# First mixer of a 1-core transformer kernel: query products moved to VectorE, one exponential for the decayed keys, pooling sums in one POOL run

## The chip, the cores and the metric

The kernel runs on one core of a Trainium2 chip. The metric is the device time of one execution in microseconds (us); the time given for a kernel is the median of its runs. The engines are TensorE (PE), VectorE (DVE), ScalarE (ACT), GpSimd (POOL) and SyncE (SP, which issues the weight loads).

## What is computed

The reference is two transformer blocks on 256 tokens of width 1024. The change lies in the first mixer of the first block, which has two halves: a causal pooling over four windows, and a gated linear recurrence with a per-channel decay.

```python
def causal_multiscale_pool(u):            # four groups of 128 channels, windows 2, 4, 8, 16
    ...
    mean = ...                            # running mean over the window, shorter at the start
    return (mean - uf).astype(u.dtype)

def even_mixer(h, w_in, pool_w, pool_scale, lb, out_gain, w_out):
    z = h @ w_in
    u, q, fz, i, g = jnp.split(z, cuts, axis=-1)
    pooled = causal_multiscale_pool(u.reshape(B_, S_, POOL_GROUPS, POOL_GROUP_DIM))
    a_out = jnp.einsum('bsgc,gcd->bsgd', pooled, pool_w).reshape(B_, S_, POOL_WIDTH) * pool_scale
    fz32 = jnp.clip(fz.astype(jnp.float32), -GATE_CLIP, GATE_CLIP)
    logf = jax.nn.log_sigmoid(fz32) + jnp.log1p(lb * jnp.exp(-fz32))
    k = (1.0 - lb) * jax.nn.sigmoid(-fz32)
    o = hgrn2_chunkwise(hs(q), hs(k), hs(i), hs(logf))
    o = rmsnorm(o, out_gain) * jax.nn.silu(hs(g))
    return jnp.concatenate([a_out, b_out], axis=-1) @ w_out
```

The recurrence's output at token t is the sum over s <= t of v[s] times the inner product of q[t] and k[s], each channel damped by exp of the sum of logf from s+1 to t. The rest of the two blocks (attention, memory attention, feed-forward parts) is untouched.

## The kernel before

Activations lie feature-major: 128 partitions by tokens. Each large product is done as three single-pass matmuls, with weights split in a high and a low part. Weights stream in groups of 128x1024 (512 KB): SP loads a group into one of 6 `raw` buffers, ACT casts it in two halves into `rhi` (line 203), DVE subtracts in two halves into `rlo` (line 241), and PE multiplies (lines 216 to 218 for a projection by columns, 24 matmuls of 256 columns a group). A ring of 7 split groups lies between the splits and PE; the split of group g + 7 becomes possible when PE is done with group g.

The code is one straight trace. A planner reads it before the launch and lays out a fixed order for each engine: at each step the instruction that comes first in the trace among those that are ready by the planner's own times. Every engine then works in its fixed order and waits by semaphores. `after(i, name)` (line 197) adds only an order on one engine. `take` (line 248) traces, before a projection, all splits that the ring allows by then, so they stand ahead of what is traced after.

`even_mixer` computes the recurrence by levels. For c = 1, 2, 4, ..., 128, the second half of each run of 2c tokens takes from the first half. `P` holds log decays summed from the run's start, `Su` those to the run's end; both are 128x1024 (four heads of 256 tokens). `level(c)` (line 724) makes the two operands: Q = exp(P) * q on the odd runs (512 columns, always in the first half of the tile `X`; the exponential on ACT, the product on POOL), and K = exp(Su) * k on the even runs (in `Y`, the exponential on ACT, the product on DVE). Level 1 uses k as it is. `masked(li, Q, K)` (line 708) multiplies them on PE (line 711, 8 products in full float32, shown as x16) and DVE copies by mask into `sT` (line 715). `advance(c)` (line 717) updates Su and P on DVE for the next level. Levels 64 and 128 have their own products (lines 814 and 822).

Beside it stand other jobs: the gate projection `gproj`, the value projection `iproj` (512-column matmuls, lines 318 to 320), the projection `uproj` of the pooling input, and jobs of the memory attention: `mem_start` (mem load, squares, high and low parts), `mem_rstd`, and key and value projections which `fill(n)` (line 538) takes one by one from a list. They are traced between the levels.

`pool_means` (line 753) makes for each of the four groups log2(w) shifted sums, each an add and a copy of the first columns on POOL, with two scratch chunks of `fz` in turn (groups 0 and 2 share one pair, 1 and 3 the other), and then two steps on DVE: a correction of the first 16 columns and the mean minus the input. It is traced between `masked(5, level(16))` and `advance(16)`. `pool_out` (line 770) multiplies the result on PE (line 777).

Elementwise calls go through helpers, so that the profile shows them under the helper's line: `tt` is line 209 (on DVE, or POOL where `self.g` is passed), `stt` line 212, `act` line 191. All units of the mixer are called `u` in the profile.

Of the kernel before, what the change touches and what calls it, by code (L numbers as in the profile page):

```python
# [11 lines left out]
AF = mybir.ActivationFunctionType  # L12
ALU = mybir.AluOpType
# [89 lines left out]
class Kern:  # L103
# [525 lines left out]
    def even_mixer(self):  # L629
        A = self.unit  # L630
        fz, q, k, sg, P, Su, Y = (A() for _ in range(7))
        X = self.maskin
        mem = self.big()
        vt, u = mem.units
        sT = A()
        cross, pw = self.ring(2, 512)
        inv, lbc = self.inv, self.lbc
# [21 lines left out]
        e4, r4, lb = lbc[:, 0:4], lbc[:, 4:8], lbc[:, 8:12]  # L659
# [4 lines left out]
        self.tt(lb, e4, e4, ALU.subtract)  # L664
        self.v.tensor_scalar(lb, lb, 0.0, 1.0, ALU.max, ALU.min)
        self.v.tensor_scalar(r4, lb, -1.0, 1.0, ALU.mult, ALU.add)
        self.g.memset(Su, 0.0)
        self.g.memset(sT, 0.0)

        ps0, ps1 = self.bank(0, 8), self.bank(0, 8)  # L670
# [10 lines left out]
        self.act(X, X, AF.Ln, bias=self.epsc[:, 1:2])  # L681
        self.stt(P, fz, 0.0, X, ALU.min, ALU.subtract)
        self.stt(Y, fz, 0.0, X, ALU.max, ALU.add)
        self.act(k, Y, AF.Exp, scale=-1.0)
        self.act(X, fz, AF.Exp, scale=-1.0)
        for h in range(4):
            c = self.chunk(X, h)
            self.act(c, c, AF.Ln, scale=lb[:, h:h + 1], bias=self.epsc[:, 1:2])
            self.v.tensor_scalar(self.chunk(k, h), self.chunk(k, h), r4[:, h:h + 1], None, ALU.mult)
        self.tt(P, P, X, ALU.add)  # L690
        psq1 = cols(512, 1)
        for j, ps in enumerate((psq0, psq1)):
# [2 lines left out]
        def runs(t, c, odd):  # L695
            return t.rearrange("p (n two c) -> p n two c", two=2, c=c)[:, :, odd]
# [10 lines left out]

        def masked(li, Q, K):
            ps = self.bank(0, 8)
            for b in range(8):  # L710
                self.pe.matmul(ps[:, b * 64:(b + 1) * 64], K[:, b * 128:(b + 1) * 128], Q[:, b * 64:(b + 1) * 64],  # L711
                               start=True, stop=True)
            c = LEVELS[li]
            V = lambda z: z.rearrange("p (n c) -> p n c", c=c)
            self.v.copy_predicated(runs(sT, c, 1), V(mk[:, li - 1]), V(ps))

        def advance(c):
            Pv = P.rearrange("p (s two c) -> p s two c", two=2, c=c)
            Sv = Su.rearrange("p (s two c) -> p s two c", two=2, c=c)
            n = 1024 // (2 * c)  # L720
            self.tt(Sv[:, :, 0], Sv[:, :, 0], Pv[:, :, 1, c - 1:c].to_broadcast([128, n, c]), ALU.add)
            self.tt(Pv[:, :, 1], Pv[:, :, 1], Pv[:, :, 0, c - 1:c].to_broadcast([128, n, c]), ALU.add)

        def level(c):

            Q = X[:, 0:512]
            Qv = Q.rearrange("p (n c) -> p n c", c=c)
            self.act(Qv, runs(P, c, 1), AF.Exp)
            self.tt(Qv, Qv, runs(q, c, 1), ALU.mult, self.g)
            if c == 1:  # L730
                return Q, k
            K = runs(Y, c, 0)
            self.act(K, runs(Su, c, 0), AF.Exp)
            self.tt(K, K, runs(k, c, 0), ALU.mult)
            return Q, Y

        def gproj(j):
# [12 lines left out]

        mh, ml = self.xh, self.xl

        def pool_means():
            for g, w in enumerate((2, 4, 8, 16)):
                src = self.chunk(u, g)
                cur = src
                sh = 1
                bufs = [self.chunk(fz, 2 * (g % 2) + i) for i in range(2)]
                i = 0
                while sh < w:  # L760
                    dst = bufs[i % 2]
                    i += 1
                    self.tt(dst[:, sh:], cur[:, sh:], cur[:, :256 - sh], ALU.add, self.g)
                    self.g.tensor_copy(dst[:, :sh], cur[:, :sh])
                    cur = dst
                    sh *= 2
                self.tt(cur[:, :16], cur[:, :16], inv[:, g * 16:(g + 1) * 16], ALU.mult)
                self.stt(src, cur, 1.0 / w, src, ALU.mult, ALU.subtract)

        def pool_out():  # L770
            pool_out1(0)
            pool_out1(1)
# [14 lines left out]
        diagonal()  # L787
        gproj(0)
        masked(1, *level(1))
        gproj(1)  # L790
        advance(1)
        iproj()
        masked(2, *level(2))
        advance(2)
        uproj(0)
        masked(3, *level(4))
        advance(4)
        uproj(1)
# [2 lines left out]
        self.mem_rstd()  # L801
        self.fill(1)
        masked(5, *level(16))
        pool_means()
        advance(16)
        self.fill(1)
        masked(6, *level(32))
        advance(32)
        self.fill(1)
        pool_out()  # L810
        Q, K = level(64)
        ps = self.bank(0, 8)
        for b in range(8):
            self.pe.matmul(ps[0:64, b * 64:(b + 1) * 64], K[:, b * 128:b * 128 + 64], Q[:, b * 64:(b + 1) * 64],
                           start=True, stop=True)
# [3 lines left out]
        Q, K = level(128)  # L819
# [22 lines left out]
        for j in range(2):  # L842
            c = slice(j * 512, (j + 1) * 512)
# [610 lines left out]
```

## Time and profile before

| | us |
|---|---|
| median of 3 runs | 1805.41 (1805.23 to 1806.15) |
| the profiled execution | 1806.07 |
| its span, first to last instruction | 1804.3 |
| PE busy in it | 1766.9 |
| DVE busy in it | 1243.2 |
| ACT busy in it | 1032.1 |
| POOL busy in it | 113.3 |

The mixer's part with the levels lies between about 44 and 126 us of the span. The page gives each engine's busy time; the waits say who waited for whom; the timeline lists the instructions of one engine in order; the windows give busy time and the granted clock of a stretch (1.00 is 2.4 GHz, 0.50 is 1.2 GHz). Ends of matmuls are modelled; starts are recorded. A row's duration overlaps the next start by about 0.1 us on DVE and ACT.

### The profile page before, as it was taken

Reading aid. Unit: us, or ns where it says so; the run is one execution under the profiler, and the core shown is the slowest. Engines: PE = TensorE matmul, PEld = TensorE weight load, DVE = VectorE, ACT = ScalarE, POOL = GpSimd, SP = SyncE. Lnnn points to the kernel's source line nnn. Section 1 sums busy time; section 2 is a strip of 40 time slices with the busy share of each in tenths; the row PEclk is TensorE's granted clock in tenths of the full one; section 3 lists DMA queues with packets and bytes.
Section 4 is the critical chain, followed back from the end, with each engine's and each line's share of the span. In section 5 each row is a group of like instructions: output and inputs, shape, how many; then the busy total and the mean of one; then the engine's idle time right before and its main releaser. Section 6 shows DMA issues by size and latency. Waiting matters only on the chain.

```text
span 1804.3 us, 36074 instructions
## 1 busy us (share of the span) xinstructions
PE 1766.9 (98%) x14406; PEld 1717.1 (95%) x14406; DVE 1243.2 (69%) x2262; ACT 1032.1 (57%) x2037; POOL 113.3 (6%) x128
## 2 busy tenths in 40 slices
PE   8899999999999999999999999999999999999997
PEld 8889999999889999999999998999999999899997
DVE  8877786557787685557656778766686666876664
ACT  7556565556566465556544667645465455775453
POOL 2420000000000000000000002000010000200000
PEclk9899999999999999999999999999999999999999
DMA  7434445554653435554555554555555555335651
GB/s 284 155 118 141 163 143 209 188 187 158 221 171 127 166 130 189 189 190 153 186 196 184 180 176 135 164 188 187 195 167 187 189 186 177 118 129 188 197 177 36
DMA packets 85625, 307.81 MB, mean 171 GB/s; under 512 B 9680, under 2 KB 10320, under 8 KB 85456
## 3 DMA queue, kind: packets, MB, share of 16 engines
q1 hardware_dynamic: 83952, 300.92, 49.3%
q0 software_dynamic: 640, 3.15, 0.6%
q8 instruction: 112, 1.84, 0.4%
q10 hardware_dynamic: 864, 1.44, 0.2%
q14 instruction: 57, 0.47, 0.1%
HBM read 304.42 MB, written 1.05 MB: 169 GB/s over the span
## 4 chain that ended last, share of the span: by engine, by line
PE 87%; DVE 6%; ACT 3%; issue 1%; POOL 1%; DMA 1%; DVEq 0%; ACTq 0%; SPq 0%; POOLq 0%
PE ps L218 25%; PE ps L216 25%; PE ps L217 25%; DVE rlo L241 2%; ACT u L191 1%; DVE u L212 1%; PE ps L318 1%; PE ps L299 1%; PE ps L300 1%; PE ps L319 1%; PE ps L320 1%; DVE u L209 1%; PE ps L298 1%; DVE xlo L212 1%; PE ps L921 1%
## 5 line engine op out<-in xcount | busy, mean ns | idle before, releaser
L203 ACT CAST rhi<-raw 128x512 fp32r<-128x512 f32 (+1 forms) x1138 | 670.0, 618 | 619.8 <-PE ps L218 582.5
L241 DVE TENSOR_TENSOR rlo<-raw,rhi 128x512 fp32r<-128x512 f32 (+1 forms) x1138 | 764.9, 697 | 328.1 <-ACT rhi L203 323.7
L216 PE MATMUL ps<-xhi,rhi 128*128 128x256 f32 x2560 | 719.9, 281 | 4.7 <-ACT xhi L191 4.0
L218 PE MATMUL ps<-xlo,rhi 128*128 128x256 f32 x2560 | 717.2, 281 | 2.5 <-DVE xlo L212 2.5
L217 PE MATMUL ps<-xhi,rlo 128*128 128x256 f32 x2560 | 715.7, 280 | 0.7 <-DVE rlo L241 0.7
L216 PEld LDWEIGHTS ps<-xhi,rhi 128*128 128x128 f32 x2560 | 482.3, 188 | 8.2 <-ACT xhi L191 5.0
L218 PEld LDWEIGHTS ps<-xlo,rhi 128*128 128x128 f32 x2560 | 481.9, 188 | 4.8 <-DVE xlo L212 4.7
L217 PEld LDWEIGHTS ps<-xhi,rlo 128*128 128x128 f32 x2560 | 482.2, 188 | 1.7 <-DVE rlo L241 1.3
L216 PE MATMUL ps<-u,rhi 128*128 128x256 f32 x1680 | 473.2, 282 | 0.0
L218 PE MATMUL ps<-u,rhi 128*128 128x256 f32 x1680 | 470.2, 280 | 0.0
L217 PE MATMUL ps<-u,rlo 128*128 128x256 f32 x1680 | 470.0, 280 | 0.0
L216 PEld LDWEIGHTS ps<-u,rhi 128*128 128x128 f32 x1680 | 316.4, 188 | 1.0 <-issue 0.7
L218 PEld LDWEIGHTS ps<-u,rhi 128*128 128x128 f32 x1680 | 316.3, 188 | 0.7 <-DVE u L206 0.6
L217 PEld LDWEIGHTS ps<-u,rlo 128*128 128x128 f32 x1680 | 316.5, 188 | 0.4 <-issue 0.2
L209 DVE TENSOR_TENSOR u<-ps,rst 128x512 f32<-128x512 f32 (+1 forms) x129 | 84.0, 656 | 102.2 <-PE ps L218 101.8
L209 POOL TENSOR_TENSOR ssum<-ssum,sqb 128x512 f32<-128x512 f32 x26 | 37.7, 1448 | 1254.0 <-ACT sqb L191 1253.8
L191 ACT ACTIVATE u<-u 128x256 f32<-128x256 f32 (+3 forms) x158 | 86.4, 548 | 36.2 <-PE ps L711 19.4
L206 DVE TENSOR_TENSOR u<-u,u 128x256 fp32r<-128x256 f32 (+2 forms) x128 | 66.7, 521 | 10.2 <-ACT u L203 8.3
L203 ACT CAST u<-u 128x256 fp32r<-128x256 f32 (+2 forms) x128 | 62.0, 484 | 11.2 <-POOL u L1186 7.3
L191 ACT ACTIVATE xhi<-xres,gain 128x256 fp32r<-128x256 f32 x96 | 43.2, 501 | 25.0 <-DVE xres L209 18.1
L212 DVE SCALAR_TENSOR_TENSOR xlo<-xres,gain,xhi 128x256 fp32r<-128x256 f32 x96 | 53.6, 587 | 2.7 <-ACT xhi L191 2.7
L209 DVE TENSOR_TENSOR u<-u,u 128x256 f32<-128x256 f32 (+2 forms) x107 | 53.8, 505 | 0.6 <-ACT u L191 0.5
(175 smaller groups left out, 1289.1 us busy)
## 6 DMA issues: line engine op xcount, KB each, us to landing
raw<-w SPq DMA_DIRECT2D x567, 512.0 KB, 4.1
u<-bias POOLq DMA_DIRECT2D x8, 384.0 KB, 3.9
xres<-x SPq DMA_DIRECT2D x4, 256.0 KB, 5.7
u<-mem ACTq DMA_DIRECT2D x4, 256.0 KB, 3.6
raw<-w SPq DMA_DIRECT2D x2, 256.0 KB, 4.7
u<-tabs SPq DMA_DIRECT2D x1, 512.0 KB, 4.2
out<-u SPq DMA_DIRECT2D x2, 256.0 KB, 2.7
u<-masks SPq DMA_DIRECT2D x1, 256.0 KB, 8.0
```

The lines of the kernel that those rows point to most:

```text
L191: i = self.a.activation(out, in_, func, scale=scale, **kw)
L203: return self.a.copy(out.bitcast(F32R), in_)
L206: return self.v.tensor_tensor(out.bitcast(F32R), in_, hi, ALU.subtract)
L209: return (eng or self.v).tensor_tensor(out, a, b, op)
L212: return self.v.scalar_tensor_tensor(out, a, s, b, op0, op1)
L216: self.pe.matmul(out, R(wh), R(xh), start=start, stop=False, skip_group_check=skip)
L217: self.pe.matmul(out, R(wl), R(xh), start=False, stop=False, skip_group_check=skip)
L218: self.pe.matmul(out, R(wh), R(xl), start=False, stop=stop, skip_group_check=skip)
L241: b = self.v.tensor_tensor(l[:, c].bitcast(F32R), r[:, c], h[:, c], ALU.subtract)
L298: self.pe.matmul(o, ah, wh, start=k == 0 and t == 0, stop=False, skip_group_check=True)
L299: self.pe.matmul(o, ah, wl, start=False, stop=False, skip_group_check=True)
L300: self.pe.matmul(o, al, wh, start=False, stop=k == 7 and t == 1, skip_group_check=True)
```

## The change

- The product of Q goes from POOL to DVE, and Q lies in the one or the other half of `X` from level to level. The name of the latest of these products is kept (`levelmul`).
- `Su` starts as log k (minus `Y` plus the logarithm of 1 - lb, made on ACT early from `r4`) instead of zero. k is one exponential of it, and K of each level one exponential of `Su` with no product. The four DVE steps that multiplied k by 1 - lb become four that write `Su`.
- `pool_means` is cut in two. `pool_sums` holds the ten adds and ten copies on POOL, traced where `pool_means` was, with a scratch chunk of its own for each group's result (and part of `cross` for the last). The eight DVE steps are traced after `advance(32)` and are ordered on DVE behind the Q product of level 32.

```diff
--- before.py
+++ after.py
@@ -664,7 +664,7 @@
         self.tt(lb, e4, e4, ALU.subtract)
         self.v.tensor_scalar(lb, lb, 0.0, 1.0, ALU.max, ALU.min)
         self.v.tensor_scalar(r4, lb, -1.0, 1.0, ALU.mult, ALU.add)
-        self.g.memset(Su, 0.0)
+        self.act(e4, r4, AF.Ln)
         self.g.memset(sT, 0.0)
 
         ps0, ps1 = self.bank(0, 8), self.bank(0, 8)
@@ -681,12 +681,12 @@
         self.act(X, X, AF.Ln, bias=self.epsc[:, 1:2])
         self.stt(P, fz, 0.0, X, ALU.min, ALU.subtract)
         self.stt(Y, fz, 0.0, X, ALU.max, ALU.add)
-        self.act(k, Y, AF.Exp, scale=-1.0)
         self.act(X, fz, AF.Exp, scale=-1.0)
         for h in range(4):
             c = self.chunk(X, h)
             self.act(c, c, AF.Ln, scale=lb[:, h:h + 1], bias=self.epsc[:, 1:2])
-            self.v.tensor_scalar(self.chunk(k, h), self.chunk(k, h), r4[:, h:h + 1], None, ALU.mult)
+            self.v.tensor_scalar(self.chunk(Su, h), self.chunk(Y, h), -1.0, e4[:, h:h + 1], ALU.mult, ALU.add)
+        self.act(k, Su, AF.Exp)
         self.tt(P, P, X, ALU.add)
         psq1 = cols(512, 1)
         for j, ps in enumerate((psq0, psq1)):
@@ -723,15 +723,15 @@
 
         def level(c):
 
-            Q = X[:, 0:512]
+
+            half = c.bit_length() % 2 * 512
+            Q = X[:, half:half + 512]
             Qv = Q.rearrange("p (n c) -> p n c", c=c)
             self.act(Qv, runs(P, c, 1), AF.Exp)
-            self.tt(Qv, Qv, runs(q, c, 1), ALU.mult, self.g)
+            self.levelmul = self.tt(Qv, Qv, runs(q, c, 1), ALU.mult).ins.name
             if c == 1:
                 return Q, k
-            K = runs(Y, c, 0)
-            self.act(K, runs(Su, c, 0), AF.Exp)
-            self.tt(K, K, runs(k, c, 0), ALU.mult)
+            self.act(runs(Y, c, 0), runs(Su, c, 0), AF.Exp)
             return Q, Y
 
         def gproj(j):
@@ -750,22 +750,27 @@
 
         mh, ml = self.xh, self.xl
 
-        def pool_means():
-            for g, w in enumerate((2, 4, 8, 16)):
-                src = self.chunk(u, g)
-                cur = src
+        spare = [self.chunk(fz, g) for g in range(4)]
+        steps = [[spare[0]], [spare[3], spare[1]], [spare[2], spare[3], spare[2]],
+                 [cross[:, 0:256], spare[3], cross[:, 0:256], spare[3]]]
+
+        def pool_sums():
+            for g in range(4):
+                cur = self.chunk(u, g)
                 sh = 1
-                bufs = [self.chunk(fz, 2 * (g % 2) + i) for i in range(2)]
-                i = 0
-                while sh < w:
-                    dst = bufs[i % 2]
-                    i += 1
+                for dst in steps[g]:
                     self.tt(dst[:, sh:], cur[:, sh:], cur[:, :256 - sh], ALU.add, self.g)
                     self.g.tensor_copy(dst[:, :sh], cur[:, :sh])
                     cur = dst
                     sh *= 2
-                self.tt(cur[:, :16], cur[:, :16], inv[:, g * 16:(g + 1) * 16], ALU.mult)
-                self.stt(src, cur, 1.0 / w, src, ALU.mult, ALU.subtract)
+
+        def pool_means():
+            for g, w in enumerate((2, 4, 8, 16)):
+                src, cur = self.chunk(u, g), spare[g]
+                a = self.tt(cur[:, :16], cur[:, :16], inv[:, g * 16:(g + 1) * 16], ALU.mult)
+                b = self.stt(src, cur, 1.0 / w, src, ALU.mult, ALU.subtract)
+                for z in (a, b):
+                    self.after(z, self.levelmul)
 
         def pool_out():
             pool_out1(0)
@@ -801,11 +806,12 @@
         self.mem_rstd()
         self.fill(1)
         masked(5, *level(16))
-        pool_means()
+        pool_sums()
         advance(16)
         self.fill(1)
         masked(6, *level(32))
         advance(32)
+        pool_means()
         self.fill(1)
         pool_out()
         Q, K = level(64)
```

## Rows read from the trace of the kernel before

**Rows 1.** The page, busy times: engine, busy us, share of the span, instructions.

```profile
PE 1766.9 (98%) x14406; PEld 1717.1 (95%) x14406; DVE 1243.2 (69%) x2262; ACT 1032.1 (57%) x2037; POOL 113.3 (6%) x128
```

**Rows 2.** Waits of PE, 44 to 126.4 us: us in total, times, longest.

```profile
PE ps L711 <- POOL u L209: 5.1, 1, 5.1
...
PE ps L711 <- DVE u L209: 3.3, 1, 3.3
...
PE ps L421 <- DVE diag L420: 1.0, 1, 1.0
```

**Rows 3.** Timeline of PE: start us, us, instruction, [idle before <- releaser].

```profile
70.29 3.68 PE L711 MATMUL ps<-u,u 128*128 128x64 f32 x16 [5.09 <-POOL u L209]
...
73.72 0.56 PE L218 MATMUL ps<-xlo,rhi 128*128 128x256 f32 x1
...
78.77 0.28 PE L217 MATMUL ps<-xhi,rlo 128*128 128x256 f32 x1
...
80.52 1.89 PE L711 MATMUL ps<-u,u 128*128 128x64 f32 x16
...
82.22 0.36 PE L217 MATMUL ps<-xhi,rlo 128*128 128x256 f32 x1
```

**Rows 4.** Timeline of PE at the other two stops.

```profile
94.33 0.70 PE L421 MATMUL ps<-diag,tabs 128*128 128x256 f32 x2 [0.95 <-DVE diag L420]
...
106.56 3.65 PE L711 MATMUL ps<-u,u 128*128 128x64 f32 x16 [3.33 <-DVE u L209]
...
109.96 0.56 PE L217 MATMUL ps<-u,rlo 128*128 128x256 f32 x1
...
112.88 0.29 PE L218 MATMUL ps<-u,rhi 128*128 128x256 f32 x1
```

**Rows 5.** Windows: us, busy us (count) of five engines, PEclk, DMA share, GB/s.

```profile
61.64:126.40 64.76, 55.25 (x408) 53.88 (x406) 51.86 (x84) 29.33 (x51) 27.49 (x27) 0.87 0.40 133
...
65.03:70.29 5.26, 0.17 (x3) 0.01 (x1) 4.07 (x7) 0.83 (x2) 5.20 (x1) 0.83 0.92 322
...
70.29:78.78 8.49, 8.49 (x40) 8.49 (x41) 4.75 (x6) 2.33 (x4) 1.75 (x1) 0.50 0.25 91
...
126.40:150.00 23.60, 23.60 (x191) 22.29 (x190) 17.38 (x29) 15.40 (x28) 0.00 (x0) 1.00 0.37 115
```

**Rows 6.** Timeline of POOL: the products of levels 2 and 32.

```profile
62.73 7.50 POOL L209 TENSOR_TENSOR u<-u,u 128x512 f32<-128x512 f32 x1 [9.60 <-ACT u L191]
...
102.36 1.28 POOL L209 TENSOR_TENSOR u<-u,u 128x512 f32<-128x512 f32 x1
```

**Rows 7.** Timeline of DVE at the stops and beside POOL's work.

```profile
61.79 4.89 DVE L241 TENSOR_TENSOR rlo<-raw,rhi 128x512 fp32r<-128x512 f32 x8
...
66.61 1.28 DVE L209 TENSOR_TENSOR u<-u,u 128x512 f32<-128x512 f32 x2
...
78.77 1.70 DVE L209 TENSOR_TENSOR u<-u,u 128x512 f32<-128x512 f32 x2
...
84.87 1.77 DVE L209 TENSOR_TENSOR u<-u,u 128x512 f32<-128x512 f32 x1
...
100.33 1.09 DVE L241 TENSOR_TENSOR rlo<-raw,rhi 128x512 fp32r<-128x512 f32 x1
...
102.43 1.24 DVE L209 TENSOR_TENSOR u<-u,inv 128x16 f32<-128x16 f32 x1 [1.01 <-POOL u L764]
...
105.73 1.28 DVE L209 TENSOR_TENSOR u<-u,u 128x512 f32<-128x512 f32 x2
```

**Rows 8.** Lines 209 and 764: duration ns min/median/max, starts, forms.

```profile
L209 DVE TENSOR_TENSOR u<-u,u x15: 675/681/1810, 46.7 to 121.7; 128x512 f32<-128x512 f32 x14, 128x1024 f32<-128x1024 f32 x1
...
L209 POOL TENSOR_TENSOR u<-u x10: 606/664/1067, 78.9 to 101.5; 128x255 f32<-128x255 f32 x4, 128x254 f32<-128x254 f32 x3, 128x252 f32<-128x252 f32 x2, 128x248 f32<-128x248 f32 x1
...
L209 POOL TENSOR_TENSOR u<-u,u x8: 1278/1719/7505, 51.4 to 121.8; 128x512 f32<-128x512 f32 x8
...
L764 POOL COPY u<-u x10: 178/288/647, 79.9 to 102.2; 128x1 f32<-128x1 f32 x4, 128x2 f32<-128x2 f32 x3, 128x4 f32<-128x4 f32 x2, 128x8 f32<-128x8 f32 x1
```

## The prediction

> **What bounds the kernel now.** I read the page first: TensorE is busy for 98% of the span [rows 1], so a change on DVE, ACT and POOL pays only where PE stands still or runs at its lower clock. The waits of PE over the stage that the diff touches name three places: a masked product that waited for POOL (5.1 us), another that waited for DVE (3.3 us), and a small product that waited for DVE (1.0 us) [rows 2]. The timeline of PE then gives what each stop costs behind the idle time.
>
> First stop, level 2. PE stands for 5.09 us before the 70.29 us row. The granted clock over the following stretch is 0.50, the lower level of 1.2 GHz [rows 5]. So the masked product and its hand-over last 73.72 - 70.29 = 3.43 us, where the next one lasts 82.22 - 80.52 = 1.70 [rows 3]: 1.7 us lost. The 23 projection matmuls from 73.72 to 78.77 take 5.05 us; at the pace of the 15 from 78.77 to 80.52 (0.117 each) they would take 2.7: 2.3 us lost. Sum 5.1 + 1.7 + 2.3 = 9.1 us.
>
> Second stop, level 32. 3.33 us idle; 109.96 - 106.56 = 3.40 us for the masked product, 1.7 too long; 14 matmuls in 112.88 - 109.96 = 2.92 us where 1.7 would do, 1.2 too long [rows 4]. Sum 6.2 us.
>
> Third, the rstd of the memory: 0.95 us idle [rows 4], with no slow matmuls behind it. All three: 9.1 + 6.2 + 1.0 = 16.3 us. From 126.4 to 150 us PE is busy throughout [rows 5], so time saved earlier should pass through to the end.
>
> Why they stop: at level 2 POOL's product of Q took 7.50 us [rows 6], against 1.28 at best [rows 8], while DVE ran from 61.79 almost without a pause [rows 7]; PE started in the moment it ended. At level 32 a short DVE step of the pooling means sat waiting for a POOL copy and then took 1.24 us beside POOL's product of Q; the K product, behind it in DVE's order, came at 105.73 [rows 7], and PE starts as it ends.
>
> **The change part by part.** *Q product to DVE, K product gone.* Levels 2 to 128 lose seven K products on DVE and gain seven Q products of the same shape, 0.68 us each [rows 8]; level 1 gains one. Net on DVE +0.7 us. POOL loses eight products of 1.28 to 7.50 us [rows 8]. DVE also loses what they cost it: five instructions between 75 and 115 us stood beside a product and were each 1.1 us longer than their kind (two of the five: 84.87, 1.77 for 0.68; 102.43, 1.24 for a step on 16 columns) [rows 7], 5.5 us in all.
>
> *What of stop one is left.* Even without POOL the K product would have held PE: the pair at 66.61 comes behind eight weight splits, and its first half ends near 67.2, 2.0 us after PE was free (70.29 - 5.09 = 65.20) [rows 3, 7]. The Q product now stands in that queue in its place, and the planner, which orders by the trace and its own times, may put it before or behind the splits: 0 to 2.0 us; I take 2.0, since the row is of the same queue. Behind it wait the splits for later weights and the updates of P and Su; who waits for those is the next level, with 38 projection matmuls to cover it.
>
> *Two buffers for Q.* The exponential of Q need no longer wait for the masked product before it. The one of K still must (Y is one buffer), so ACT's queue still holds weight casts behind that wait. Worth nothing by itself while projections cover a level; bounds 0 to -1 us, I take 0.
>
> *One exponential for decayed keys.* Four DVE steps are replaced by four of the same size; the exponential for k moves behind four logarithms on ACT, so the diagonal's product may be ready up to 1.5 us later (bounds 0 to 1.5). Gate projections cover it; uncovered it would cost that 1.5. The extra logarithm on a 4-wide tile and the dropped memset lie early: 0.
>
> *Pooling sums.* The same ten adds and ten copies, about 10 x 0.66 + 10 x 0.29 = 9.5 us of POOL [rows 8], now without DVE steps between them. POOL holds nothing else then, so they should start when u is there and end well before the output product. Before, five DVE instructions beside them were longer by 0.25 to 0.5 us, 2.0 us in all (first and last: 78.77, 100.33) [rows 7]. Packed into one run, 2.0 to 3.0; I add 1.0.
>
> *DVE's eight steps of the means* go behind level 32's Q product: stop two loses its cause. In its place the output product waits for the eight steps, about 2.4 us, and 47 projection matmuls (5.5 us) stand before it. I take the 6.2 us as gained whole; if the cover fails, up to 2.4 comes back. No DMA is moved, and SP's queue only follows PE.
>
> *Third stop:* its chain of tiny DVE steps stays, now beside the sums: 0 to 2 us, I keep 1.0.
>
> **DVE's room.** Between 61.64 and 126.4 us DVE is busy 51.9 of 64.8 us [rows 5]. After: 51.9 - 5.5 = 46.4, of PE's 64.8 - 16.3 = 48.5. That is 96%: it fits, but any lateness of DVE against the plan shows on PE. Hence my remainders 2.0 + 1.0 + 1.0 = 4.0 us, in gaps short enough to keep the clock as the third stop did.
>
> Sum: 16.3 - 4.0 = 12.3 us gained. The profiled execution is 1806.1 us with a span of 1804.3, 0.7 over the median of 1805.4; the saving is taken off the median: 1793.
>
> **A rule weighed.** Rows: POOL's sums took only 2.0 us from DVE, while a product beside them took 1.1 each time [rows 7]. The Trainium skill (SBUF — State Buffer, section Who interferes with whom) says that when a DVE instruction with two SBUF inputs meets a GpSimd instruction that reads SBUF, whichever starts first holds the shared port for its whole length and the other fully blocks. By that rule the packed run could cost DVE its whole length, which is the first rival; rows 7 bear it out for the long products, for the short sums only in part.
>
> **The rivals.**
> 1. *DVE becomes the bound.* If the run of sums costs DVE all of its 9.5 us instead of the 2.0 contained in the 46.4, DVE needs 53.9 us where PE needs 48.5: 5.4 us of idle PE over my remainder of 3.0 without the sums, 8.4 in all: 1805.4 - 16.3 + 8.4 = 1797.5. If one gap falls long enough for the lower clock, as 3.33 us did, another 2.9 (1.7 + 1.2) follow: 1800.4. For it: 96%; against it: 2.0 us measured. I name 1799, 25%.
> 2. *Given back.* PE leaves the stage earlier, with a less filled ring of split weights (in stop one DVE and the DMA, 0.92 busy [rows 5], caught up), and waits for weights instead: no change, 1805. Against it: DMA is at 0.40 over the stage [rows 5] and PE's waits there name no weight. 12%.
> 3. *Slower.* Each masked product of levels 1 to 32 now needs DVE in its order, behind splits traced earlier. If DVE is late by over 3 us at such a level, PE stops as at level 32 for 6.2 us. Three stops (18.6) outweigh 16.3; four give 1805.4 - 16.3 + 24.8 = 1814. For it: eight splits stood ahead in the 61.79 row; against: PE has projections to run in the meantime and the plan knows DVE's order. 8%.
> 4. *All gone.* Nothing of the remainders comes: 1805.4 - 16.3 = 1789, or below with shorter tails elsewhere. 5%, apart from the forecast.
>
> **How the numbers follow.** Forecast 50%, 1789 to 1797. The likeliest is 1793. For 8 in 10 the range takes the forecast, rival 4 and rival 1: 1787 to 1801. A measurement tells about 0.2%, 3.6 us, from no change: faster means under 1801.8: 0.50 + 0.05 + nearly all of 0.25 = 0.79; same 0.12 plus a little of rival 1, 0.13; slower 0.08.
>
> **What would show it.** Right: no wait of a masked product for POOL; the waits of PE between 44 and 115 us sum to 3 to 5 us; granted clock near 1.00 over the stage; the span from 61.64 us to the level-128 product (line 822) near 52 us instead of 64; the sums on POOL end before level 32. Wrong: a masked product that waits over 3 us for the Q product on DVE, with 0.5 of clock behind it (rivals 1, 3); the output product waiting for the means; projections waiting for weight splits (rival 2).

## Result and profile after

The changed kernel takes 1794.01 us, the median of 6 runs (1792.51 to 1795.24), where the kernel before took 1805.56 on the same chip (6 runs, 1804.42 to 1809.04): a ratio of 0.9932, 95% interval 0.9922 to 0.9942. That is 11.6 us faster by the medians; the forecast was 12.3 off the median, 1793. The profiled execution took 1794.85 with a span of 1793.0, 11.3 less than the span before.

The page after: busy us, share, instructions of each engine, to set beside [rows 1].

```profile
PE 1762.4 (98%) x14406; PEld 1712.9 (96%) x14406; DVE 1236.9 (69%) x2263; ACT 1032.4 (58%) x2038; POOL 96.4 (5%) x119
```

TensorE has the same 14406 matmuls and is busy for 4.5 us less. The matmuls that no longer run at the lower clock behind the two stops are worth 6.9 us of it by the prediction's sums (1.7 + 2.3 + 1.7 + 1.2); 2.5 us come back in later stages (the table below). The waits of PE over the stage, 44 to 125 us (us in total, times, longest):

```profile
PE ps L711 <- DVE u L209: 1.6, 2, 1.2
PE ps L421 <- DVE diag L420: 0.8, 1, 0.8
PE ps L703 <- DVE u L209: 0.3, 1, 0.3
PE ps L711 <- issue: 0.2, 1, 0.2
```

Against [rows 2], the wait for POOL (5.1) and the long one for DVE (3.3) are gone; what is left sums to 2.9 us. The timeline of PE shows where it lies (start, us, instruction, idle before and its releaser; levels 1, 2, 4, 8, then the rstd of the memory, the factor that normalises it, then level 16):

```profile
57.42 2.00 PE L711 MATMUL ps<-u,u 128*128 128x64 f32 x16 [1.17 <-DVE u L209]
...
66.80 1.97 PE L711 MATMUL ps<-u,u 128*128 128x64 f32 x16 [0.20 <-issue]
...
73.72 2.00 PE L711 MATMUL ps<-u,u 128*128 128x64 f32 x16 [0.47 <-DVE u L209]
...
79.80 1.89 PE L711 MATMUL ps<-u,u 128*128 128x64 f32 x16
...
87.13 0.70 PE L421 MATMUL ps<-diag,tabs 128*128 128x256 f32 x2 [0.84 <-DVE diag L420]
...
88.60 1.67 PE L711 MATMUL ps<-u,u 128*128 128x64 f32 x14
```

Level 2, where PE stood 5.09 us [rows 3], now waits 0.20. Level 1, where PE didn't wait before, waits 1.17. The wait at L703 (0.3) is that of the product of the diagonal, before level 1. No masked product takes the 3.68 or 3.65 us that it took behind the two stops [rows 3, 4]. DVE over the same stretch, and POOL at the start of the stage and at the last step of the sums:

```profile
50.40 3.37 DVE L212 SCALAR_TENSOR_TENSOR u<-u,gain,u 128x256 fp32r<-128x256 f32 x3
...
54.30 1.26 DVE L212 SCALAR_TENSOR_TENSOR u<-u,gain,u 128x256 fp32r<-128x256 f32 x3
...
56.68 0.68 DVE L209 TENSOR_TENSOR u<-u,u 128x512 f32<-128x512 f32 x1
...
61.21 4.88 DVE L241 TENSOR_TENSOR rlo<-raw,rhi 128x512 fp32r<-128x512 f32 x8
66.01 1.28 DVE L209 TENSOR_TENSOR u<-u,u 128x512 f32<-128x512 f32 x2
...
72.96 1.72 DVE L209 TENSOR_TENSOR u<-u,u 128x512 f32<-128x512 f32 x2
...
87.00 1.69 DVE L209 TENSOR_TENSOR u<-u,u 128x512 f32<-128x512 f32 x2
```

```profile
50.55 2.94 POOL L209 TENSOR_TENSOR ssum<-ssum,sqb 128x512 f32<-128x512 f32 x2 [25.97 <-ACT sqb L191]
73.15 0.99 POOL L209 TENSOR_TENSOR u<-u 128x255 f32<-128x255 f32 x1 [19.66 <-DVE u L209]
...
90.01 0.19 POOL L763 COPY u<-u 128x8 f32<-128x8 f32 x1
```

Read three things here. The Q product of level 2 (66.01, a pair) still stands behind eight splits, as the K product did [rows 7]. The Q product of level 1 (56.68) comes late because three DVE steps of normally 1.26 us (54.30) took 3.37 us beside two of POOL's adds for the memory's squares (50.40 and 50.55). And the sums run on POOL from 73.15 to 90.2 us, before level 32. The windows after, for [rows 5] (us, busy us and count of PE, PEld, DVE, ACT, POOL, then PEclk, DMA share, GB/s):

```profile
61.20:112.00 50.80, 49.29 (x409) 47.71 (x408) 45.63 (x83) 30.41 (x51) 13.08 (x20) 1.00 0.48 158
```

The stretch to the product of level 128 is 50.8 us where it was 63.9 (61.64 to 125.57), the clock is at its upper level throughout, and DVE is busy 90% of it.

To follow the gain through the kernel, take the first product of the row of rstd values (L447) behind each later stage as a mark (five of sixteen):

| mark, us | before | after | after less before |
|---|---|---|---|
| end of the mixer | 165.39 | 151.73 | -13.66 |
| | 643.50 | 629.85 | -13.65 |
| | 662.33 | 649.57 | -12.76 |
| | 830.96 | 819.80 | -11.16 |
| last one | 1792.67 | 1781.42 | -11.25 |

The stage gains 13.7 us; 2.5 of these are missing at the end, lost in two places some 480 us and more behind the change. These are single executions: the changed kernel, profiled a second time, has its first mark at 152.23, so marks of two executions of one kernel can lie 0.5 us apart.

### The profile page after: what moved, and what is told of

It is laid out like the page before. It is cut to its first block, busy times and chain, and to the rows that moved or that the text cites. A ratio compares the mean times of both kernels' runs of the same rounds, so it can differ in the third digit from the quotient of the medians.

```text
span 1793.0 us, 36042 instructions
## 1 busy us (share of the span) xinstructions
PE 1762.4 (98%) x14406; PEld 1712.9 (96%) x14406; DVE 1236.9 (69%) x2263; ACT 1032.4 (58%) x2038; POOL 96.4 (5%) x119
## 4 chain that ended last, share of the span: by engine, by line
PE 89%; DVE 6%; ACT 3%; issue 1%; DMA 1%; POOL 0%; DVEq 0%; SPq 0%; ACTq 0%
PE ps L218 26%; PE ps L216 26%; PE ps L217 25%; DVE rlo L241 2%; ACT u L191 1%; PE ps L319 1%; PE ps L320 1%; PE ps L318 1%; PE ps L299 1%; PE ps L300 1%; PE ps L298 1%; PE ps L927 1%; PE ps L945 1%; ACT rhi L203 1%; PE ps L447 1%
## 5 line engine op out<-in xcount | busy, mean ns | idle before, releaser
L191 ACT ACTIVATE u<-u 128x256 f32<-128x256 f32 (+3 forms) x158 | 86.5, 548 | 23.9 <-DVE u L209 11.6
L203 ACT CAST u<-u 128x256 fp32r<-128x256 f32 (+2 forms) x128 | 62.0, 484 | 11.3 <-POOL u L1192 7.3
L191 ACT ACTIVATE xhi<-xres,gain 128x256 fp32r<-128x256 f32 x96 | 43.2, 502 | 24.0 <-DVE xres L209 17.3
```

What stands on the lines that cost most here:

```text
L191: i = self.a.activation(out, in_, func, scale=scale, **kw)
L203: return self.a.copy(out.bitcast(F32R), in_)
```

## Experiments

Each is compared with the kernel before on the same chip (1806.16 us for the first four, 1805.11 for the next four, 1807.32 for the last four). "Mark" is the end of the mixer as in the table above; 165.39 is the kernel before, 151.73 the changed one.

### The sums and means alone

```diff
 # kernel before
-            self.tt(K, K, runs(k, c, 0), ALU.mult)
+            self.levelmul = self.tt(K, K, runs(k, c, 0), ALU.mult).ins.name
-        pool_means()
+        pool_sums()
         advance(16)
 ...
         advance(32)
+        pool_means()
```

> The kernel before with one part of the change alone: the pooling sums in one POOL run and DVE's eight steps behind level 32 (ordered behind its K product, since Q's stays on POOL). Theory, two separate causes: the stop at level 32 (6.2 us) goes, the stop at level 2 (9.1 us) stays: 1798 to 1801 us. Rival, POOL's products cause both stops: less than 2 us gained, 1804 or more, with an idle PE of about 3 us at level 32 left.

Measured: 1806.74 us, ratio 1.0003 (0.9994 to 1.0012), mark 164.96. Nothing is gained; the expectation of the theory missed. The rival had the time right and named POOL's products, but expected the stop at level 32. PE, then POOL:

```profile
70.02 3.67 PE L711 MATMUL ps<-u,u 128*128 128x64 f32 x16 [4.98 <-POOL u L209]
...
97.61 3.68 PE L711 MATMUL ps<-u,u 128*128 128x64 f32 x16 [2.94 <-POOL u L209]
...
109.15 1.89 PE L711 MATMUL ps<-u,u 128*128 128x64 f32 x16
```

```profile
62.47 7.50 POOL L209 TENSOR_TENSOR u<-u,u 128x512 f32<-128x512 f32 x1 [8.81 <-ACT u L191]
...
96.15 0.19 POOL L763 COPY u<-u 128x8 f32<-128x8 f32 x1
96.30 1.26 POOL L209 TENSOR_TENSOR u<-u,u 128x512 f32<-128x512 f32 x1
```

The stop at level 32 is indeed gone (109.15, no wait). But the Q product of level 16 now stands in POOL's queue behind the packed sums, and PE stops there for it, with the slow masked product behind. Here the packed run moved the stop and did not remove it.

### The Q products on DVE alone

```diff
 # kernel before
-            self.tt(Qv, Qv, runs(q, c, 1), ALU.mult, self.g)
+            self.tt(Qv, Qv, runs(q, c, 1), ALU.mult)
```

> The kernel before with the Q products on DVE alone: one buffer, K product and pooling as before. Theory: the stop at level 2 shrinks from 9.1 to 2 or 3 us since only DVE's lateness is left of it; the stop at level 32 stays, since the K product still stands behind the pooling steps: 1797 to 1801 us. Rival, DVE is the bound: the eight added products (4.9 us of DVE) show on PE and nothing is gained, 1804 or more.

Measured: 1800.41 us, 0.9965 (0.9951 to 0.9979), mark 158.54. PE, then DVE ahead of the stop, then windows:

```profile
57.35 2.32 PE L711 MATMUL ps<-u,u 128*128 128x64 f32 x16 [1.23 <-DVE u L209]
69.08 1.89 PE L711 MATMUL ps<-u,u 128*128 128x64 f32 x16
...
104.07 3.64 PE L711 MATMUL ps<-u,u 128*128 128x64 f32 x16 [3.84 <-DVE u L209]
```

```profile
97.88 0.18 DVE L209 TENSOR_TENSOR u<-u,inv 128x16 f32<-128x16 f32 x1 [1.90 <-POOL u L764]
...
100.41 0.17 DVE L209 TENSOR_TENSOR u<-u,inv 128x16 f32<-128x16 f32 x1 [1.01 <-POOL u L764]
...
102.64 1.89 DVE L209 TENSOR_TENSOR u<-u,u 128x512 f32<-128x512 f32 x3
```

```profile
57.00:61.00 4.00, 3.65 (x20) 3.36 (x21) 3.12 (x6) 0.00 (x0) 0.00 (x0) 0.73 0.41 130
61.00:65.00 4.00, 4.00 (x19) 3.26 (x17) 4.00 (x8) 1.59 (x3) 0.00 (x0) 0.84 0.58 153
```

Stop one is gone by this part alone; the stop at level 32 stays, and now no product of POOL is in it: DVE waited 1.90 and 1.01 us for POOL's copies of the means, and the products of Q and K stand behind (102.64, with a third step). A new wait of 1.23 at level 1 is followed by a lower clock (0.73, 0.84).

### The changed kernel with Q on POOL

```diff
 # changed kernel; the order of the means is tied to the P update of advance(16)
-            self.levelmul = self.tt(Qv, Qv, runs(q, c, 1), ALU.mult).ins.name
+            self.tt(Qv, Qv, runs(q, c, 1), ALU.mult, self.g)
```

> The changed kernel with the Q products back on POOL (all other parts kept; the pooling steps on DVE ordered behind level 16's update of P). Theory: POOL's product starves again beside DVE's splits, a PE stop of 4 to 6 us with the lower clock behind it at one level at least: 1801 to 1805 us. Rival, the K product on DVE was the true cause of the stop at level 2: no long wait for POOL, 1794 to 1796.

Measured: 1803.67 us, 0.9985 (0.9976 to 0.9994), mark 161.23. Of the stage's 13.7 us only 4.2 are left, and PE waits for POOL at level 2 again:

```profile
66.99 3.68 PE L711 MATMUL ps<-u,u 128*128 128x64 f32 x16 [4.57 <-POOL u L209]
...
94.10 0.70 PE L421 MATMUL ps<-diag,tabs 128*128 128x256 f32 x2 [2.13 <-DVE diag L420]
```

```profile
86.50 1.27 POOL L209 TENSOR_TENSOR u<-u,u 128x512 f32<-128x512 f32 x1 [1.35 <-ACT u L191]
89.00 0.99 POOL L209 TENSOR_TENSOR u<-u 128x255 f32<-128x255 f32 x1 [1.23 <-DVE u L209]
```

This is as the theory expected. No masked product waits behind the packed sums here, although the Q products stand in POOL's queue with them: the Q product of level 16 (86.50) came ahead of the last seven adds (from 89.00), where in the first experiment it came behind them (96.30). What moved it, the second buffer for Q or the dropped K product, was not tested.

### The changed kernel with the K product kept

```diff
 # changed kernel
-        self.act(e4, r4, AF.Ln)
+        self.g.memset(Su, 0.0)
...
+        self.act(k, Y, AF.Exp, scale=-1.0)
...
-            self.v.tensor_scalar(self.chunk(Su, h), self.chunk(Y, h), -1.0, e4[:, h:h + 1], ALU.mult, ALU.add)
-        self.act(k, Su, AF.Exp)
+            self.v.tensor_scalar(self.chunk(k, h), self.chunk(k, h), r4[:, h:h + 1], None, ALU.mult)
...
-            self.act(runs(Y, c, 0), runs(Su, c, 0), AF.Exp)
+            K = runs(Y, c, 0)
+            self.act(K, runs(Su, c, 0), AF.Exp)
+            self.tt(K, K, runs(k, c, 0), ALU.mult)
```

> The changed kernel with K as exponential and product again (seven more DVE products of 0.68 us, 4.2 us at DVE's pace, Su from zero). Theory: DVE was busy 45.6 of 50.8 us between the start of level 1's update and level 128, so most of the 4.2 us shows: PE waits in 44 to 115 us rise from 2.9 to 5 or 7 us, 1796 to 1799. Rival, DVE has room enough: 1793 to 1795.

Measured: 1795.27 us, 0.9944 (0.9929 to 0.9958), mark 152.99, 1.3 behind the changed kernel's and 0.8 behind that of its second execution. The interval overlaps that of the changed kernel. Waits of PE, 44 to 125 us, and the windows behind level 1:

```profile
PE ps L711 <- DVE u L209: 1.8, 3, 1.2
PE ps L421 <- DVE diag L420: 0.6, 1, 0.6
```

```profile
57.00:61.00 4.00, 3.79 (x21) 3.39 (x22) 3.45 (x7) 0.16 (x1) 0.00 (x0) 0.79 0.39 131
61.00:65.00 4.00, 4.00 (x18) 3.27 (x17) 4.00 (x8) 1.59 (x3) 0.00 (x0) 0.78 0.66 178
```

The waits sum to 2.4 us, not more than the 2.9 of the changed kernel: DVE has room for seven more products. The difference lies in one place, the lower clock behind the wait of 1.2 us at level 1 (9 matmuls of 512 columns in 3.72 us, where 0.234 each would be 2.1). The changed kernel waits 1.17 there and keeps 1.00.

### One buffer, no sums, the means early, the memory's adds on DVE

Four kernels on one chip, each the changed kernel with one edit. One buffer for Q:

```diff
-            half = c.bit_length() % 2 * 512
+            half = 0
```

> The changed kernel with Q in one buffer for all levels. Theory: 0, since the exponential of K waits for the masked product before it in any case and projections cover the level: 1793 to 1795 us. Rival, the second buffer takes DVE's Q product off the chain between two masked products: 1 us or more at two or three levels, 1796 to 1798.

Measured: 1793.96 us, 0.9937 (0.9922 to 0.9952), mark 151.50. In the changed kernel the second buffer is worth nothing that can be told: the marks of the changed kernel are 151.73 and 152.23.

No pooling sums on POOL:

```diff
-                src, cur = self.chunk(u, g), spare[g]
+                src = cur = self.chunk(u, g)
...
-        pool_sums()
```

> The changed kernel with the ten adds and ten copies of the pooling sums on POOL left out; DVE's eight steps read the input itself, so the pooled half is not the reference's. Theory: beside DVE's work the run costs PE 1 us at most, 1793 to 1794.5. Rival, each sum holds DVE up for its whole length: 4 us or more are gained, below 1790.

Measured: 1792.37 us, 0.9929 (0.9915 to 0.9944), mark 151.32. Two of DVE's steps, for the 72.96 and 87.00 rows above:

```profile
73.25 1.29 DVE L209 TENSOR_TENSOR u<-u,u 128x512 f32<-128x512 f32 x2
...
86.41 1.29 DVE L209 TENSOR_TENSOR u<-u,u 128x512 f32<-128x512 f32 x2
```

Five DVE steps beside the sums are 1.8 us longer in the changed kernel than here (these two by 0.43 and 0.40). PE's wait for the rstd of the memory (0.84) is gone, and its mark is 0.4 before the changed kernel's first execution and 0.9 before the second. So the whole run of sums costs the path up to 0.9 us. The median is 1.5 us below those of the kernels with one buffer and with the means early (1793.96, 1793.82) on the same chip, but the runs overlap.

The means' eight steps traced behind the sums again, with no order on DVE:

```diff
-                for z in (a, b):
-                    self.after(z, self.levelmul)
...
         pool_sums()
+        pool_means()
         advance(16)
...
         advance(32)
-        pool_means()
```

> The changed kernel with DVE's eight pooling steps traced behind the sums again and without the order behind level 32's Q product. Theory: in the changed kernel the last sum ends on POOL at 90.2 us, 2 us before level 32's Q product; in the plan it ends sooner, so DVE waits in its order for POOL and PE stops at level 16 or 32 for 1 to 4 us: 1796 to 1801 us. Rival, with Q on DVE the place of the steps is of no account: 1793 to 1795.

Measured: 1793.82 us, 0.9934 (0.9917 to 0.9950), mark 152.07. The theory missed. The steps did move on DVE, to 87.81 from 95.36, and the Q product of level 32 came at 95.43 where it came at 92.35; but PE had projections until then, and the product of level 32 doesn't wait. With the sums packed, the place of the steps is of no account.

The adds of the memory's squares on DVE:

```diff
-        self.tt(self.ssum, self.ssum, q, ALU.add, self.g if b < 3 else None)
+        self.tt(self.ssum, self.ssum, q, ALU.add, self.g if b < 3 and not dve else None)
...
-            self.square2(b, mem[:, b * 512:(b + 1) * 512])
+            self.square2(b, mem[:, b * 512:(b + 1) * 512], True)
```

> The changed kernel with the two adds of the memory's squares on DVE in place of POOL. In the changed kernel three DVE steps beside them took 3.37 us for 1.2 (from 50.40 us), and level 1's product on PE waits 1.17 us for the Q product on DVE behind them. Theory: two adds of 0.6 us cost less than the 2.1 us that the lock takes, the wait at level 1 falls by 0.9: 1792.5 to 1794. Rival, the wait at level 1 is set by the plan and not by this: no change, or 1 us slower for the added DVE work.

Measured: 1791.14 us, 0.9924 (0.9910 to 0.9939), mark 150.28. The wait at level 1 is gone and the stage ends 1.4 us earlier than in the changed kernel's first execution, although DVE has two adds more. The median lies below the range of the theory, 2.7 to 2.8 us below those of the kernels with one buffer and with the means early on the same chip; the kernel was run again (below). The kernel with one buffer gives a step between: there the two adds cost DVE 1.5 us, and level 1 waits 0.58.

### The old pooling in the changed kernel

```diff
 # changed kernel; pool_means as it was before, shared scratch, DVE's steps between the sums
-        pool_sums()
+        pool_means()
         advance(16)
...
         advance(32)
-        pool_means()
```

> The changed kernel with the pooling of before: sums and DVE steps interleaved with shared scratch, traced before level 16's update, no order behind level 32. Theory, after the run with the steps early alone gained and lost nothing: it is the packed run, not the place of the steps, that removed the stop at level 32; with the interleaved form DVE waits for POOL ahead of level 32's Q product and PE stops there for 2 to 4 us: 1796 to 1801 us. Rival, the stop came from POOL's product of Q standing behind the sums, which is gone: 1793 to 1795.

Measured: 1798.30 us, 0.9953 (0.9939 to 0.9967), mark 155.26: 3.8 us behind the changed kernel run beside it (below), and the stage 3.0 behind. PE, a window behind it with the lower clock (0.72), DVE and POOL:

```profile
97.90 1.97 PE L711 MATMUL ps<-u,u 128*128 128x64 f32 x16 [2.15 <-DVE u L209]
```

```profile
101.00:105.00 4.00, 4.00 (x27) 4.00 (x27) 2.13 (x5) 1.34 (x3) 0.00 (x0) 0.72 0.37 134
```

```profile
94.23 0.17 DVE L209 TENSOR_TENSOR u<-u,inv 128x16 f32<-128x16 f32 x1 [1.01 <-POOL u L764]
...
97.07 1.29 DVE L209 TENSOR_TENSOR u<-u,u 128x512 f32<-128x512 f32 x2
```

```profile
88.66 0.61 POOL L209 TENSOR_TENSOR u<-u 128x255 f32<-128x255 f32 x1 [6.58 <-DVE u L212]
```

POOL's sums of the third group need the scratch that a DVE step frees, and wait 6.58 us for it; DVE's correction then waits 1.01 us for POOL, and the products of level 32 stand behind it. In the kernel with the means early, which has the steps as early but the sums in one run with scratch of their own, neither queue waits for the other and the product of level 32 doesn't wait; the mark is 152.07. The kernel with the Q products on DVE alone has this pooling too, and differs from this one by the K product and the single buffer: there PE waits 3.84 us at level 32, the masked product takes 3.64 us instead of 1.97, and the mark is 158.54, 3.3 us later. So with the old pooling the dropped K products are worth more than with the new one.

### The changed kernel again, and two steps further

Three kernels beside the last one on its chip: the changed kernel unchanged, the one with the memory's adds on DVE again, and that one with the rstd of the memory traced earlier:

```diff
 # kernel with the memory's adds on DVE
         advance(2)
+        self.mem_rstd()
         uproj(0)
...
-        self.mem_rstd()
         self.fill(1)
         masked(5, *level(16))
```

> The changed kernel as it is, beside the others on one chip. From its runs: 1792.5 to 1795.5 us. If the steady pace of matmuls in a stage changes from execution to execution, its profile differs from the first one by steps of about 1.6 us between the same points; if the pace belongs to the program, the points agree within 0.1 us.

> The changed kernel with the two adds of the memory's squares on DVE, again, on the same chip as the changed kernel. Up to the end of the mixer its first profile was 1.4 us ahead of the changed kernel's: 1 to 2 us below the changed kernel's median. Rival: within 0.5 us of it, since what is saved at level 1 returns at the rstd of the memory and level 16.

> The adds of the memory's squares on DVE, and the rstd of the memory traced before the first projection of the pooling input instead of before the first key projection. Theory: its chain of small DVE steps then runs before POOL's sums begin, and the 0.97 us wait of PE for it falls below 0.4: about 0.6 us faster than with the adds on DVE alone. Rival: the planner puts the small product as tightly as before and the same wait comes earlier: no difference.

Measured: 1794.47 us (0.9930, 0.9918 to 0.9943; mark 152.23), 1793.23 (0.9925, 0.9913 to 0.9938; 150.30) and 1791.81 (0.9914, 0.9901 to 0.9928; 149.32). The last one's PE at the rstd of the memory, and what is left of waits in its stage, 44 to 125 us:

```profile
71.81 0.70 PE L421 MATMUL ps<-diag,tabs 128*128 128x256 f32 x2 [0.37 <-DVE diag L420]
```

```profile
PE ps L421 <- DVE diag L420: 0.4, 1, 0.4
PE ps L711 <- ACT rhi L203: 0.3, 1, 0.3
```

All its runs (1789.95 to 1792.96) lie below all runs of the changed kernel beside it (1793.76 to 1795.55): 2.7 us by the medians, 2.9 by the marks. It is the fastest of the kernels run on that chip, ahead of both kernels of the change. Against the kernel with the adds on DVE alone the rstd's wait falls as expected, from 0.94 to 0.37, and the mark by 1.0. That kernel's second run is 1.2 us below the changed kernel by the medians, at the low end of what was expected (1 to 2); their runs overlap, the marks differ by 1.9. The changed kernel beside them is 12.9 us below the kernel before.

## Why the prediction was right, and where its steps were not

**The three stops** were priced at 16.3 us, with 2.9 us of new or remaining waits the stage should gain 13.4; the mark shows 13.7, and 13.2 in the second execution. So the price of a stop as idle time plus slow masked product plus slow matmuls behind it holds. It holds for stop one apart from the rest, too: Q on DVE alone should gain 9.1, and the third stop's 1.0 which is gone there, less its new waits of 1.2 and 0.3, the 0.5 by which it waits longer at level 32, and 1.4 of lower clock behind level 1 (7 matmuls of 512 columns in 3.01 us from 59.43 to 62.44, where 0.234 each would be 1.64): 6.7 us. Its mark shows 6.9.

**Stop one, its cause.** POOL's product beside DVE's unbroken run is what held PE: moved alone it ends the stop, moved back it brings it back (4.57 us). Shown both ways.

**What of stop one is left** was put at 2.0 us at level 2, behind eight splits. The order on DVE came as feared (61.21, 66.01), but level 2 waits 0.20 only: DVE started on the splits 0.6 us earlier than before (61.21 against 61.79), and PE was free for the product at 66.80 - 0.20 = 66.60, 1.4 later than before, most of it the new wait at level 1. The remainder lies one level earlier, at level 1: 1.17 us, from POOL's adds of the memory's squares, which the prediction did not list among POOL's work there. Taking them off POOL removes it. The place and cause were wrong; that the size (1.4 for 2.0) came near is luck. The waits at level 4 (0.47) and at the diagonal (0.3) were not in the sum either.

**Stop two.** The prediction said that it "loses its cause" because DVE's eight steps go behind level 32. That step failed: traced early again, the steps cost nothing measurable (1793.82 us). What held DVE was in part the to and fro between POOL and DVE over shared scratch: with the steps as early in both, the kernel with the old pooling ends the stage 3.2 us later than the one with the packed sums. The other part goes with the K product, which stood in the same queue: with it, the old pooling and one buffer for Q, PE waits 3.84 us at level 32 instead of 2.15. The 6.2 us came all the same, since the diff did all of this at once. The prediction also took the parts as separable. They are coupled: Q on DVE alone gains 5.8 us, packing alone nothing, both 10.9 (the kernel with the K product kept), because in the kernel with packing alone the Q product of level 16 stood in POOL's queue behind the run. Taking the Q products off POOL rules that out. It is not the only way: in the changed kernel with Q on POOL that product came ahead of the run, and the stops left are those at level 2 and at the rstd of the memory.

**The sums beside DVE.** Forecast 2.0 to 3.0 us on DVE and 1.0 on the path; measured 1.8 on DVE and 0.4 to 0.9 on the path. As it turned out the sum counts one wait twice: the 1.0 for the sums and the 1.0 for the third stop are both the wait for the rstd, which is 0.84 and gone without the sums. Rival 1 rested on the rule of the Trainium skill (SBUF — State Buffer, Who interferes with whom) that the later instruction fully blocks. For these sums the trace does not bear out the rival's price: POOL was busy 13.1 us in the stretch and DVE lost 1.8. Most of the delay fell on POOL: at the shortest forms seen there (0.61 us an add, 0.18 a copy) ten of each would take 7.9 us, an estimate. At the start of the stage it bears out more: two adds on 512 columns, 2.94 us long, cost three DVE steps 2.1 us.

**One exponential, two buffers.** Two buffers: 0, as forecast. The K products: forecast as room on DVE (96% busy), and the rest of the argument leaned on it. Measured, DVE is busy 90%, and with the products kept the waits are no longer. What their removal brought, with Q on DVE and the sums packed, is 0.8 to 1.3 us of clock behind level 1, seen in one execution of the one and two of the other; the medians do not tell them apart. With the old pooling it brought, together with the second buffer, 3.3 us, at level 1 and level 32. The later exponential for k, bounded at 0 to 1.5 us, cost a wait of 0.3 at the diagonal.

**DVE's room, given back, slower.** DVE's busy time in the stretch was forecast at 46.4 us and is 45.6. What the prediction wanted to see came out nearly throughout: no masked product that waits for POOL, a clock of 1.00, 50.8 us to the product of level 128 (near 52), the sums ended at 90.2 before level 32, and waits of 2.9 us (3 to 5). The output product does not wait for the means. No projection waits for a weight in the stage, so rival 2 falls as it was put; no masked product waits for over 1.2 us, so rival 3 falls.

**From 13.7 to 11.6.** The stage came out 1.4 us better than the 12.3 forecast, the whole 0.7 worse by the medians; in the second pair of runs the whole was 12.9. The step that is not borne out is the one that lets time saved in the stage "pass through to the end", as if the later stages took the same time in every execution: two of them differ by 0.9 and 1.6 us between executions or kernels that do not touch them (last section), together more than separates 13.7 from 11.6. That the median fell within 1 us of the forecast is in part luck, with a stage mis-sized one way and the later stages the other.

## What to carry over

Price a stop as the idle time plus what the lower clock behind it costs, and read what stands in the queues on both sides of it: an operation on the critical path doesn't belong on an engine that another's work holds up (7.50 us for a product of 1.28) or whose queue holds a long run ahead of it. When work is packed into one run on a helper engine, see that what the main engine waits for is out of that queue or ahead of the run; packing alone only moved the stop from level 32 to level 16. When two in-order engines hand a scratch buffer to and fro, give each step its own buffer before moving its place in the order, since here, with buffers of their own, the place did nothing to the time.

## What the hardware showed beyond the expectation

**The same wait, with and without a lower clock.** Around 640 us PE waits 1.74 us for ACT in all kernels. Windows of the kernel before, of the changed kernel, and of the changed kernel run again:

```profile
643.00:653.90 10.90, 9.16 (x57) 7.74 (x56) 9.62 (x22) 6.11 (x13) 0.97 (x1) 1.00 0.28 98
```

```profile
629.40:640.30 10.90, 9.16 (x47) 7.74 (x46) 9.62 (x22) 6.16 (x13) 1.03 (x1) 0.89 0.29 98
640.30:650.30 10.00, 10.00 (x82) 9.95 (x81) 9.04 (x16) 6.16 (x14) 2.05 (x2) 0.95 0.01 2
```

```profile
629.80:640.70 10.90, 9.16 (x57) 7.73 (x56) 9.63 (x22) 6.19 (x13) 1.06 (x1) 1.00 0.29 98
```

The busy times are alike to 0.1 us, yet the clock fell in one execution of the changed kernel (0.89, then 0.95) and not in the other. That is 0.9 us of the 2.5 missing, and it belongs to the execution, not to the change: the stretch from 643.50 to 662.33 before, 18.8 us, is 19.7 to 19.8 in four of the fourteen profiled executions, the changed kernel once and three variants of it, and 18.8 in the others. At level 1, too, waits of 1.16 to 1.26 us kept 1.00 in five executions of kernels with the one exponential (the changed kernel twice, no sums, means early, old pooling), while the clock fell in both kernels that have Q on DVE and keep the K product (0.73 and 0.79). In those two the product of the diagonal starts at 43.2 to 43.3 us, in the five at 45.9 to 46.3. What decides is open.

**Two steady paces at one clock.** From 662.33 to 830.96 the kernel before takes 168.63 us, the changed one from 649.57 to 819.80 takes 170.23, with the same matmuls, no wait of PE and a granted clock of 1.00 in both: 116.7 and 117.8 ns from one start to the next, the mean over 1437 of them. The changed kernel run again shows 170.23 again; with one buffer for Q the stretch ran at the faster pace. The kernel with one buffer, then the changed kernel, in the same window (431 matmuls recorded in 50 us, against 426):

```profile
650.00:700.00 50.00, 50.00 (x431) 50.00 (x430) 34.68 (x56) 29.48 (x53) 0.00 (x0) 1.00 0.62 212
```

```profile
650.00:700.00 50.00, 50.00 (x426) 50.00 (x425) 34.34 (x56) 29.75 (x53) 0.00 (x0) 1.00 0.61 207
```

The kernel with the memory's adds on DVE had the slower pace in a second stage in one execution and not in the other. In the stretch from 662.33 three of the fourteen profiled executions took 168.63 us (the kernel before, one buffer, means early) and the other eleven 170.23, among them the kernel before with one part of the change alone, twice. So the 1.6 us, the rest of what is missing, can't be put down to the change: the kernel before was profiled once, and in this stage it had the rarer, faster pace. Which pace a stage gets was not settled.
